# Accumulating DMAs issued from GpSimd in place of VectorE subtractions and sums, in a hybrid encoder layer

## The chip, the cores and the metric

The kernel runs on one core of a Trainium2 chip. The metric is the device time of one execution in microseconds (us), the median of several runs. Beside the runs there is one profiled execution, from which all durations below come.

The engines are TensorE (PE; its weight loads are listed apart as PEld), VectorE (DVE), ScalarE (ACT), GpSimd (POOL) and SyncE (SP, which here issues DMAs only). Each works through its own queue of instructions in order; an instruction that waits for a semaphore holds up everything behind it in that queue.

## The reference, cut to what matters

One layer over 512 tokens of width 1024: a combined input projection, three token mixers with a gated merge, an output projection, and a gated feed-forward network, all in float32.

```
h = rms_norm(x, norm_mix)
proj = h @ w_in                      # pool | lru | q | k | v | 3 gates, 1024 columns each
y_pool = pool_mixer(u_pool); y_lru = rglru_mixer(u_lru)
y_sb = stick_breaking_attention(rms_norm(q), rms_norm(k), v)
merged = sum over the branches b of sigmoid(g_b + b_gate) * (y_b @ w_branch[b])
x = x + merged @ w_out
x = x + (silu(h2 @ w_ffn_gate) * (h2 @ w_ffn_up)) @ w_ffn_down      # h2 = rms_norm(x, norm_ffn)
```

## The kernel before, in words

**Split products.** The operands of the products have the type float32r (`F32R`, fp32r in the rows). Each is split into a high part, the value written in that type, and a low part, what is left of it; a product is then three matmuls, high x high, high x low and low x high (`mm3`, L225). For weights this is `split_w` (L97): ScalarE copies the raw tile into `whi` (L100), VectorE subtracts `whi` from the raw tile into `wlo` (L101). A tile holds 128 x 1024 values, 512 KB.

**Weight tiles and buffers.** All weights up to the feed-forward network go through one list, `specs`: each entry loads a raw tile from memory (SyncE's queue), splits it and hands the two parts to the products. The pool `wp` has three buffers for each of `raw`, `whi` and `wlo`, and `weights` (L218) keeps three entries ahead of the products. So a new high part waits until TensorE is done with the tile three entries back, and a new raw load waits until the split three entries back has read its buffer. `emit_next` (L209) gives these loads and splits a higher priority than the code around them; a scheduler then puts the instructions of each engine into a fixed order when the program is built. What is moved or added in one place can therefore change the order of others, on any engine.

**The q, k and v products.** They use a scheme with seven products in place of eight (Strassen in Winograd's form). For each of q, k and v (`t` = 0, 1, 2) the weights are cut into four blocks 11, 12, 21, 22, and the seven left operands are, in `ORDER` (L130): 11, 12, S2, S1, S3, S4, 22. S3 = 11 - 21, S2 = 22 - S3, S1 = 21 + 22, S4 = 12 - S2. Each block comes in two halves (`i`), so there are fourteen tiles for each `t`, twelve matmuls for each tile. The raw blocks lie in buffers of their own (`qraw`, eight buffers of the tag `w`); S3, S1 and S4 are formed in place of their first operand, S2 in a buffer of another tag. `SUMS_AT` (L153) says at which of the fourteen tiles each sum is written into the program. `qkv_sum` (L144) forms them on VectorE (L149). The results of a product are collected on ScalarE and VectorE (`snap` L718, `final` L722). For q and k a root follows: a sum of squares on VectorE (`ssq`, L679, L680), a power on GpSimd (`rsqq`, L255), four short VectorE operations (L256 to L259), and for k eight scalings on ScalarE (L694). The tensors then go to memory from GpSimd's queue (`qd`, L671), as the gates (`gd`, L502) and the recurrence (`yd`, L613) do. Half chunks of the third gate are mixed in between the products.

**Pool, attention and branches.** Here the eight attention heads run as small tasks between the chunks of the pool and branch products. A branch product (`branch` L862, and L1007 for the third) multiplies a mixer's output by `w_branch`: three branches, four chunks of 256 columns, two half chunks each, so 24 weight tiles, each with 24 matmuls (`half_chunk`, L276). They are entered by `add_branch` (L118) through `add_chunk256` (L111) and `add_direct` (L104).

The functions that the change touches, and what calls them:

Of the kernel before, what the change touches and what calls it, by code (L numbers as in the profile page):

```python
# [8 lines left out]
F32 = mybir.dt.float32  # L9
F32R = mybir.dt.float32r  # L10
BF16 = mybir.dt.bfloat16
AF = mybir.ActivationFunctionType
ALU = mybir.AluOpType
# [3 lines left out]
P = 128  # L17
# [46 lines left out]
def layer_kernel(ctx: ExitStack, tc: tile.TileContext, x, xt, vecs, w_in, w_pool, w_rg, w_ig,  # L64
                 w_branch, w_out, w_fg, w_fu, w_fd, out):
    nc = tc.nc
    act = nc.scalar.activation
# [13 lines left out]
    def b4(shape, name, tag="b", dt=F32):  # L81
        bufs = {"w": NAW, "t": NAT, "b": NAB}[tag]
        return pools["ap0"].tile([P] + shape, dt, tag=tag, name=name, bufs=bufs)
# [5 lines left out]
    def cols(ap, k0, nk, c0, nc_):  # L89
        return ap[k0 * P:(k0 + nk) * P, c0:c0 + nc_].rearrange("(k p) c -> p k c", p=P)  # L90


    def weight_tiles(nh, nl, o=0):
        return [wp.tile([P, 1024 + 128], F32R, tag=tag, name=n)[:, o:o + 1024]
                for tag, n in (("whi", nh), ("wlo", nl))]

    def split_w(raw, shape, n):  # L97
        hi, lo = (t.rearrange("p (a b) -> p a b", a=shape[1])
                  for t in weight_tiles("whi" + n, "wlo" + n))
        act(hi, raw, AF.Copy)  # L100
        dve.tensor_tensor(lo, raw, hi.bitcast(F32), ALU.subtract)  # L101
        return hi, lo

    def add_direct(key, src, a, b):  # L104
        def make(n):
            raw = wp.tile([P, a, b], F32, tag="raw", name="raw" + n)
            nc.sync.dma_start(raw, src)
            return split_w(raw, [P, a, b], n)
        specs.append((key, make))

    def add_chunk256(key, ap, c0):  # L111
        add_direct(key + (0,), cols(ap, 0, 4, c0, 256), 4, 256)
        add_direct(key + (1,), cols(ap, 4, 4, c0, 256), 4, 256)
# [18 lines left out]
    CH = {"11": 0, "12": 0, "21": 1, "22": 1}  # L132
    KH = {"11": 0, "12": 1, "21": 0, "22": 1}
    qraw = {}

    def qkv_raw(t, nm, i):
        if (t, nm, i) not in qraw:
            qraw[t, nm, i] = r = b4([2, 512], f"qw{t}{nm}{i}", "w")
            nc.sync.dma_start(r, cols(w_in, 4 * KH[nm] + 2 * i, 2, 2048 + t * 1024 + CH[nm] * 512, 512))
        return qraw[t, nm, i]  # L140

    def qkv_sum(t, nm, i):  # L144
        x, y, op = {"S3": ("11", "21", ALU.subtract), "S2": ("22", "S3", ALU.subtract),
                    "S1": ("21", "22", ALU.add), "S4": ("12", "S2", ALU.subtract)}[nm]
        x, y = qkv_raw(t, x, i), qkv_raw(t, y, i)
        r = b4([2, 512], f"qs{t}{i}") if nm == "S2" else x
        dve.tensor_tensor(r, x, y, op)  # L149
        qraw[t, nm, i] = r  # L150
# [5 lines left out]
    def add_seven(t, nm, i):  # L156
        def make(n):
            p = 2 * ORDER.index(nm) + i
            if p < 4:
                qkv_raw(t, nm, i)  # L160
            h, l = None, None
            if p == 1:
                h, l = split_w(qraw[t, nm, i], [P, 2, 512], n)
            if p in SUMS_AT:
                qkv_sum(t, *SUMS_AT[p])
            return (h, l) if h is not None else split_w(qraw[t, nm, i], [P, 2, 512], n)
        specs.append((("seven", t, nm, i), make))
# [6 lines left out]
    for n in range(4):  # L174
        add_direct(("first", n), cols(w_in, 2 * n, 2, 5120, 512), 2, 512)
# [158 lines left out]
    with ExitStack() as first:  # L334
# [379 lines left out]
        for t in range(3):  # L714
            ps = {}
            r = {}
# [301 lines left out]
    with ExitStack() as ffn:  # L1018
# [3 lines left out]
        def g4(shape, name, dt=F32):  # L1022

            return gp.tile([P] + shape, dt, tag="g", name=name)
# [13 lines left out]
        for c in range(4):  # L1038
# [5 lines left out]
            for j in range(2):  # L1044
# [3 lines left out]
                t = x1p[c // 2, j][:, c % 2, :]  # L1048
# [77 lines left out]
        CH = {"11": 0, "12": 0, "21": 1, "22": 1}  # L1126
        KH = {"11": 0, "12": 1, "21": 0, "22": 1}
# [3 lines left out]
        raw = {}  # L1131
# [81 lines left out]
        for c in range(NDIRECT):  # L1213
# [4 lines left out]
            a = g4([2, S], f"act{c}")  # L1218
# [26 lines left out]
        for m in range(4):  # L1245
            t = fp.tile([P, 2, S], F32, tag="mm", name=f"ps_d{m}")
# [38 lines left out]
        for kc in range(KD, last + 1):  # L1285
            split_act(kc + 1)
            ah, al = split.pop(kc)
            for e in range(2):
# [3 lines left out]
                for j in range(4):  # L1292
# [5 lines left out]
                    if kc == last:  # L1298
                        t = x1[m]
# [8 lines left out]
        for q in range(2):  # L1308
# [4 lines left out]
            lo, hi, full = slice(0, H), slice(H, S), slice(0, S)  # L1313
# [50 lines left out]
```

## Time and profile before

| what | value |
|---|---|
| median of 3 runs | 936.94 us (936.89 to 939.02) |
| profiled execution: its own time | 936.89 us |
| profiled execution: span from first to last instruction | 934.8 us |
| granted TensorE clock, mean | 0.999 |
| DMA packets | 124.13 MB, mean 133 GB/s |

A view with groups gives line, engine, operation, out<-in by the program's names, shapes and count, then the busy time in us and the mean of one in ns, then the idle time of the engine just before them and what ended it. A timeline row gives start and duration in us, then the instruction; the bracket gives the idle time before it and the releaser. A DMA issue's row ends with the median time from issue to landing. A row of the chain that ended last gives start, duration and a run of instructions. Matmuls overlap, and their ends are modelled, so a wait of TensorE is a little longer than the idle time shown.

### The profile page before, as it was taken

To read this page: it belongs to the slowest core of one execution; us is meant where nothing else is said; L and a number is where in the kernel's file an instruction comes from. 1 tells how busy PE (TensorE), PEld (TensorE's weight loads), DVE (VectorE), ACT (ScalarE), POOL (GpSimd) and SP (SyncE) were. 2 spreads that over 40 slices of the span, in tenths; PEclk is the share of its full clock that TensorE was granted. 3 is DMA by queue.
4 is the path that set the end of the run, shared out by engine and by line. 5 is a ranking of instruction groups with operands and counts; after the bars stand their busy time and mean duration, and the time that the engine had idled before them with its cause. 6 is when DMAs were issued, how large, how long until landed. Compare 5 with 4: busy or idle time off the path is not lost.

```text
span 934.8 us, 13035 instructions
## 1 busy us (share of the span) xinstructions
PE 922.3 (99%) x5089; PEld 793.8 (85%) x5089; DVE 709.8 (76%) x889; ACT 485.7 (52%) x657; POOL 44.4 (5%) x69
## 2 busy tenths in 40 slices
PE   9999999999999999999999999999999999999998
PEld 6887787787878888788788878889999999988898
DVE  6897599786686698867865545699888888787465
ACT  6636977545574556645633324454555555653232
POOL 2000000322211000000000000000000000000000
PEclk9999999999999999999999999999999999999999
DMA  9574352743614933255532344355433334533001
GB/s 336 157 263 125 105 189 68 246 137 117 199 72 150 292 113 106 89 157 173 145 100 84 100 135 135 93 149 143 135 92 104 101 110 135 164 100 103 1 29 63
DMA packets 126894, 124.13 MB, mean 133 GB/s; under 512 B 7408, under 2 KB 105712, under 8 KB 126832
## 3 DMA queue, kind: packets, MB, share of 16 engines
q1 hardware_dynamic: 122800, 108.87, 38.0%
q0 software_dynamic: 3888, 14.16, 4.4%
q8 instruction: 40, 0.66, 0.3%
q10 hardware_dynamic: 144, 0.26, 0.1%
q14 instruction: 22, 0.18, 0.1%
HBM read 107.02 MB, written 16.25 MB: 132 GB/s over the span
## 4 chain that ended last, share of the span: by engine, by line
PE 86%; DVE 7%; ACT 2%; issue 2%; POOL 2%; DMA 0%; SPq 0%; POOLq 0%; DVEq 0%; ACTq 0%
PE ps_y L1176 11%; PE ps_x L1176 8%; PE ps_br L226 5%; PE ps_br L228 4%; PE ps_br L227 4%; PE ps_q L708 4%; PE ps_d L226 3%; PE ps_d L228 3%; PE ps_d L227 3%; PE ps_gate L226 2%; PE ps_gate L227 2%; PE ps_gate L228 2%; PE ps_dy L1176 2%; PE ps_gate L627 2%; DVE wlo L101 2%
## 5 line engine op out<-in xcount | busy, mean ns | idle before, releaser
L100 ACT ACTIVATE whi<-raw 128x1024 fp32r<-128x1024 f32 x93 | 98.4, 1058 | 150.0 <-PE ps_br L227 46.2
L101 DVE TENSOR_TENSOR wlo<-raw,whi 128x1024 fp32r<-128x1024 f32 x93 | 113.5, 1221 | 65.4 <-ACT whi L100 60.3
L1166 ACT ACTIVATE wh_S<-w_S 128x1024 fp32r<-128x1024 f32 x44 | 46.6, 1061 | 56.5 <-PE ps_y L1176 25.6
L1167 DVE TENSOR_TENSOR wl_S<-w_S,wh_S 128x1024 fp32r<-128x1024 f32 x44 | 53.6, 1221 | 12.8 <-ACT wh_S L1166 12.6
L1166 ACT ACTIVATE wh<-w 128x1024 fp32r<-128x1024 f32 x33 | 35.0, 1062 | 49.1 <-issue 13.2
L101 DVE TENSOR_TENSOR wlo<-qw,whi 128x1024 fp32r<-128x1024 f32 x36 | 43.9, 1221 | 17.0 <-ACT whi L100 16.9
L1167 DVE TENSOR_TENSOR wl<-w,wh 128x1024 fp32r<-128x1024 f32 x33 | 40.3, 1222 | 17.4 <-ACT wh L1166 17.4
L100 ACT ACTIVATE whi<-qw 128x1024 fp32r<-128x1024 f32 x36 | 38.0, 1055 | 23.6 <-PE ps_q L708 15.0
L226 PE MATMUL ps_gate<-HH,whi 128*128 128x512 f32 x128 | 50.2, 392 | 0.0
L227 PE MATMUL ps_gate<-HL,whi 128*128 128x512 f32 x128 | 49.8, 389 | 0.0
L228 PE MATMUL ps_gate<-HH,wlo 128*128 128x512 f32 x128 | 49.8, 389 | 0.0
L226 PE MATMUL ps_d<-ah,whi 128*128 128x512 f32 x112 | 43.7, 391 | 0.0
L227 PE MATMUL ps_d<-al,whi 128*128 128x512 f32 x112 | 43.6, 389 | 0.0
L228 PE MATMUL ps_d<-ah,wlo 128*128 128x512 f32 x112 | 43.6, 389 | 0.0
L1154 DVE TENSOR_TENSOR w_S<-w,w 128x1024 f32<-128x1024 f32 x22 | 26.9, 1223 | 3.3 <-PE ps_d L227 2.9
L226 PEld LDWEIGHTS ps_gate<-HH,whi 128*128 128x128 f32 x128 | 24.0, 188 | 5.6 <-issue 0.7
L228 PEld LDWEIGHTS ps_gate<-HH,wlo 128*128 128x128 f32 x128 | 24.0, 188 | 5.0
L227 PEld LDWEIGHTS ps_gate<-HL,whi 128*128 128x128 f32 x128 | 24.0, 188 | 4.9
L1154 DVE TENSOR_TENSOR w_S<-w,w_S 128x1024 f32<-128x1024 f32 x22 | 26.9, 1223 | 0.6
L929 DVE TENSOR_TENSOR_SCAN E<-K,zero 128x511 f32<-128x511 f32 (+3 forms) x32 | 25.5, 811 | 1.1 <-ACT K L924 1.1
L226 PE MATMUL ps_out<-mth,whi 128*128 128x512 f32 x64 | 25.0, 390 | 0.9 <-DVE g L311 0.9
L226 PE MATMUL ps_br<-yph,whi 128*128 128x512 f32 x64 | 25.6, 400 | 0.0
(633 smaller groups left out, 3004.7 us busy)
## 6 DMA issues: line engine op xcount, KB each, us to landing
raw<-in_w_in_dram SPq DMA_DIRECT2D x39, 512.0 KB, 4.7
qw<-in_w_in_dram SPq DMA_DIRECT2D x24, 512.0 KB, 5.0
raw<-in_w_branch_dram SPq DMA_DIRECT2D x24, 512.0 KB, 3.5
w<-in_w_ffn_gate_dram SPq DMA_DIRECT2D x36, 256.0 KB, 3.7
w<-in_w_ffn_up_dram SPq DMA_DIRECT2D x36, 256.0 KB, 4.3
raw<-in_w_ffn_down_dram SPq DMA_DIRECT2D x14, 512.0 KB, 3.6
qd<-r POOLq DMA_DIRECT2D x12, 512.0 KB, 3.4
at<-qd SPq DMA_DIRECT2D x24, 256.0 KB, 5.1
```

Source lines behind the costliest of these rows:

```text
L100: act(hi, raw, AF.Copy)
L101: dve.tensor_tensor(lo, raw, hi.bitcast(F32), ALU.subtract)
L226: nc.tensor.matmul(ps, lh, rh, start=start, stop=False, skip_group_check=skip)
L227: nc.tensor.matmul(ps, lh, rl, start=False, stop=False, skip_group_check=skip)
L228: nc.tensor.matmul(ps, ll, rh, start=False, stop=stop, skip_group_check=skip)
L627: nc.tensor.matmul(pss[n // 2][n % 2], w[:, k % 2, n * P:(n + 1) * P], hu[k][x_], start=k == 0 and w is wh and x_ == 0, stop=k == KT - 1 a ...
L708: nc.tensor.matmul(ps[:, a, :], b_[:, k, ts_], a_[:, kk, :], start=first and n == k == 0, stop=n == 2 and k == 3, skip_group_check=True)
L929: dve.tensor_tensor_scan(E[:, f - 1:c0 + n - 1][:, ::-1], K[:, f:c0 + n][:, ::-1], zero[:, 0:1].to_broadcast([P, c0 + n - f]), 1.0, ALU.mu ...
L1154: dve.tensor_tensor(t, raw[c, x], raw[c, y], op)
L1166: act(h, raw[c, nm], AF.Copy)
L1167: dve.tensor_tensor(l, raw[c, nm], h.bitcast(F32), ALU.subtract)
L1176: nc.tensor.matmul(o, a[:, w, k, :], b[:, k, :], start=first and n == k == 0, stop=n == 2 and k == 3, skip_group_check=True)
```

## The change

A new function, `split_d`, makes a weight tile's two parts without VectorE. ScalarE writes the high part, then writes its negative into the low part's buffer; a DMA from GpSimd's queue then adds the raw tile to it in place (`accum_op`), so that the buffer ends as raw - high. `add_direct` uses it for the entries whose key begins with `br`, the 24 branch tiles; all others keep `split_w`.

In `qkv_sum`, S1 = 21 + 22 is no longer a VectorE addition of two raw blocks: a DMA from GpSimd's queue reads block 22 from memory and adds it to the buffer of block 21. Block 22 is still loaded as before, for S2 and for its own product. There are six such tiles, two for each of q, k and v. The other three sums stay on VectorE.

```diff
+    def split_d(raw, shape, n):
+        hi, lo = (t.rearrange("p (a b) -> p a b", a=shape[1])
+                  for t in weight_tiles("whi" + n, "wlo" + n))
+        act(hi, raw, AF.Copy)
+        act(lo, hi.bitcast(F32), AF.Copy, scale=-1.0)
+        nc.gpsimd.dma_start(lo, raw, accum_op=ALU.add)
+        return hi, lo
+
     def add_direct(key, src, a, b):
         def make(n):
             raw = wp.tile([P, a, b], F32, tag="raw", name="raw" + n)
             nc.sync.dma_start(raw, src)
-            return split_w(raw, [P, a, b], n)
+            return (split_d if key[0] == "br" else split_w)(raw, [P, a, b], n)
         specs.append((key, make))
...
     def qkv_sum(t, nm, i):
+        if nm == "S1":
+            qraw[t, nm, i] = r = qkv_raw(t, "21", i)
+            src = cols(w_in, 4 * KH["22"] + 2 * i, 2, 2048 + t * 1024 + CH["22"] * 512, 512)
+            nc.gpsimd.dma_start(r, src, accum_op=ALU.add)
+            return
         x, y, op = {"S3": ("11", "21", ALU.subtract), "S2": ("22", "S3", ALU.subtract),
-                    "S1": ("21", "22", ALU.add), "S4": ("12", "S2", ALU.subtract)}[nm]
+                    "S4": ("12", "S2", ALU.subtract)}[nm]
```

## The prediction

> **What bounds the kernel now.** I read the page's totals first, then the busy time of two stretches, then the waits of TensorE, then the timeline around each of them. In the stretches the columns are the time, then the busy us of TensorE, of its weight loads, of VectorE, ScalarE and GpSimd; in the waits who waited for whom, the us in total, how often, the longest.
>
> ```profile
> span 934.8 us, 13035 instructions
> ...
> PE 922.3 (99%) x5089; PEld 793.8 (85%) x5089; DVE 709.8 (76%) x889; ACT 485.7 (52%) x657; POOL 44.4 (5%) x69
> ...
> q0 software_dynamic: 3888, 14.16, 4.4%
> ```
> ```profile
> 131.00:300.00 169.00, 165.19 (x722) 134.82 (x721) 132.87 (x155) 104.19 (x135) 35.52 (x32) 1.00 0.44 146
> 300.00:545.00 245.00, 243.34 (x1208) 200.90 (x1207) 177.10 (x272) 118.83 (x201) 0.00 (x0) 1.00 0.46 135
> ```
> ```profile
> PE ps_q L708 <- DVE wlo L101: 3.0, 3, 1.4
> ...
> PE pw L943 <- DVE ypl L838: 0.9, 1, 0.9
> ...
> PE ps_q1S L708 <- DVE wlo L101: 0.8, 2, 0.5
> ```
>
> TensorE is busy for 922.3 of 934.8 us, and its instructions don't change. So the change acts only through idle time of TensorE: what it takes away, or what it adds. In the stretch of the q, k and v products (131 to 300) TensorE is idle for 169.0 - 165.2 = 3.8 us, and the waits say why: 3.0 + 0.8 us for a low part (wlo) that VectorE delivers late. In the whole pool, attention and branch stretch (300 to 545) it is idle for 245.0 - 243.3 = 1.7 us, and no wait in the whole list names the low part of a branch weight. VectorE is the busiest helper in both (132.9 of 169, 177.1 of 245), but only in the first does it hold TensorE up.
>
> **Part one: the branch weights' low parts.** Each of the 24 half chunks now costs VectorE one subtraction; the change puts a second ScalarE activation (the negated high part) and one accumulating DMA from GpSimd in its place.
>
> ```profile
> L101 DVE TENSOR_TENSOR wlo<-raw,whi 128x1024 fp32r<-128x1024 f32 x93 | 113.5, 1221 | 65.4 <-ACT whi L100 60.3 <-PE pq L892 5.0
> L100 ACT ACTIVATE whi<-raw 128x1024 fp32r<-128x1024 f32 x93 | 98.4, 1058 | 150.0 <-PE ps_br L227 46.2 <-PE ps_out L227 26.0 <-PE ps_d L227 21.1
> 421.61 1.06 ACT L100 ACTIVATE whi<-raw 128x1024 fp32r<-128x1024 f32 x1 [4.38 <-PE ps_br L227]
> 427.05 1.06 ACT L100 ACTIVATE whi<-raw 128x1024 fp32r<-128x1024 f32 x1 [4.38 <-PE ps_br L227]
> 422.71 1.23 DVE L101 TENSOR_TENSOR wlo<-raw,whi 128x1024 fp32r<-128x1024 f32 x1 [4.21 <-ACT whi L100]
> qd<-r POOLq DMA_DIRECT2D x12, 512.0 KB, 3.4
> gd<-gt POOLq DMA_DIRECT2D x11, 512.0 KB, 5.4
> ```
>
> VectorE loses 24 x 1.22 = 29.3 us of its 177.1; ScalarE gains, at the price of the high part's row, 24 x 1.06 = 25.4 us on its 118.8; GpSimd, empty here (the second stretch's 0.00), gains 24 issues. None of the three becomes the bound of 245 us. What matters is the time from the high part to the landed low part. The two ScalarE rows show the tight rhythm: each high part starts when TensorE lets go of the buffer three tiles back (the releaser), and the next follows after 427.05 - 421.61 = 5.44 us, one tile on TensorE (24 matmuls, 0.227 us each). With three buffers the tile whose high part starts at T is due at T + 2 x 5.44, and its low part two matmuls later, at T + 11.3. Until now it is ready at 422.71 + 1.23 - 421.61 = 2.3 us after T. Afterwards ScalarE is through both activations at 2 x 1.06 = 2.1, 2.3 with a hand-over like the one to VectorE, and 9.0 us are left for the DMA from issue to landing.
>
> The trace has no accumulating DMA. Below, it can't beat a plain store of the same 512 KB from GpSimd, 3.4 us; above, I take the slower of the two store rows twice, 2 x 5.4 = 10.8. A plain GpSimd DMA keeps 16 engines busy for 4.4% x 934.8 / 27 issues (12 + 11 on the rows here, four more yd stores) = 1.5 us; reading a second operand adds that once more, so I take 3.4 + 1.5 = 5, nearer to the lower row because the branch stretch's queues are not crowded. It is hidden under two tiles of matmuls: 0 us on the path. The bounds: under 9.0 nothing, at 10.8 a rival below.
>
> Two queues wait with it. The raw buffer is let go when the DMA has read it, some 4 us later than now, and SyncE's next branch load, with the gate, head and recurrence loads behind it, starts that much later. And what stands behind a negation on ScalarE comes 1.06 us later.
>
> ```profile
> 501.34 16.75 SPq L107 DMA_DIRECT2D raw<-in_w_branch_dram  x4
> raw<-in_w_branch_dram SPq DMA_DIRECT2D x24, 512.0 KB, 3.5
> 371.25 1.06 ACT L100 ACTIVATE whi<-raw 128x1024 fp32r<-128x1024 f32 x1
> 373.28 0.69 ACT L895 ACTIVATE qkh<-pq,vt 128x512 fp32r<-128x512 f32 x1 [0.97 <-PE py L227]
> ```
>
> Four such loads are issued over 16.75 us, one a tile; a buffer comes round in three tiles, 16.3 us, less 2.3 for the split and 3.5 for the load: 10.5 us to spare, so 4 cost nothing. ScalarE's tightest place is near 373, ahead of the two short waits of TensorE behind the pooling; there the negation falls into 0.97 us in which ScalarE waits for TensorE (py) anyway: 371.25 + 2 x 1.06 = 373.4 in place of 373.3. Without that cover it would cost its 1.06. I take 0.
>
> The Trainium skill, "Collectives: The Full Stack", section on the bandwidth ceiling, says an adding DMA isn't slowed by its adder but by its two source reads on one ring, which halves its rate. No run here shows it yet. By that rule the 1.5 us would become 3.0, the sum would stay as it is, and a late landing would be less likely than I put it below.
>
> **Part two: the S1 sums.** Six of the twelve additions and differences of this row leave VectorE, 6 x 1.22 = 7.3 us; six accumulating DMAs read the second operand from memory once more.
>
> ```profile
> L149 DVE TENSOR_TENSOR qw<-qw,qw 128x1024 f32<-128x1024 f32 x12 | 14.5, 1219 | 0.1
> 263.88 11.20 PE ps_q L708 x47
> 280.52 5.44 PE ps_q L708 x24
> ```
>
> Their landing is covered: a tile of these products takes TensorE 5.44 / 2 = 2.72 us, and the tightest of the six, the second of v, is issued near 261 and due five tiles after the v tile at 263.1 to 263.9, near 276.7: 15 us, beyond even the 10.8. What costs is the order. In the changed program, set beside the old one engine by engine, VectorE, ScalarE and GpSimd have another order, and each runs its queue strictly in turn. So I replayed by hand the four places where TensorE waits for a low part, with the old durations; a long VectorE operation follows the last at 1.14 us (208.40 after 207.26, below).
>
> ```profile
> 150.23 1.22 DVE L101 TENSOR_TENSOR wlo<-qw,whi 128x1024 fp32r<-128x1024 f32 x1
> 167.30 1.22 DVE L603 TENSOR_TENSOR ls<-ls,li 128x1024 f32<-128x1024 f32 x1
> 168.43 1.21 DVE L101 TENSOR_TENSOR wlo<-qw,whi 128x1024 fp32r<-128x1024 f32 x1
> 173.67 1.22 DVE L101 TENSOR_TENSOR wlo<-qw,whi 128x1024 fp32r<-128x1024 f32 x1
> 167.48 3.69 POOL L255 TENSOR_TENSOR rsqq<-ssq,mhalf 128x8 f32<-128x8 f32 x1 [3.66 <-DVE ssq L680]
> 272.09 1.66 POOL L255 TENSOR_TENSOR rsqq<-ssq,mhalf 128x8 f32<-128x8 f32 x1 [10.90 <-DVE ssq L680]
> ```
>
> First, q's second tile (low part at 150.23, TensorE waits until it ends): a sum leaves the stretch ahead of it, but the second of the two products of L602 moves up into the gap; five long operations stand ahead before and after. 0 us.
>
> Second, q's first S3 tile (low part at 173.67). The root on GpSimd (L255) takes 1.66 us while VectorE does nothing long, but here 3.69, ending 1.5 us after VectorE's last two-operand operation (171.17 against 168.43 + 1.21 = 169.64). In the new order the low part that was at 168.43 stands behind the wait for that root and a scan: root done near 170, scan to 171.3, low part done at 172.5 and due at 170.7, 1.8 us late, the next another 0.25. 2.05 us in place of 1.55 (the longest wait, 1.4, and what the modelled ends hide): +0.5.
>
> ```profile
> 207.26 1.22 DVE L149 TENSOR_TENSOR qw<-qw,qs 128x1024 f32<-128x1024 f32 x1
> 208.40 1.21 DVE L101 TENSOR_TENSOR wlo<-qw,whi 128x1024 fp32r<-128x1024 f32 x1
> 223.61 2.16 ACT L694 ACTIVATE r<-r,krs 128x128 f32<-128x128 f32 x7 [3.20 <-DVE krs L259]
> ```
>
> Third, k's S1 tiles (0.8 shown). A wait for a root now stands ahead of the low part at 208.40 too, just behind S4's sum (207.26, by the relief now at 206.4): root done at 207.6 + 1.5 = 209.1, low part at 209.3. The relief is gone again, and three of the eight scalings (L694) now stand before the S1 tile's high part on ScalarE. I get the low part at 225.0, due 224.0, and 0.5 more on the next, against 1.1 today: +0.5.
>
> ```profile
> 256.87 1.22 DVE L101 TENSOR_TENSOR wlo<-qw,whi 128x1024 fp32r<-128x1024 f32 x1
> 258.90 1.25 ACT L501 ACTIVATE gt<-ps_gate,vt 128x512 f32<-128x512 f32 x2
> 263.54 1.06 ACT L100 ACTIVATE whi<-qs 128x1024 fp32r<-128x1024 f32 x1 [1.66 <-PE ps_q L708]
> 264.51 1.00 ACT L720 ACTIVATE r<-ps_q 128x1024 f32<-128x1024 f32 x1
> 273.71 0.75 POOL L671 DMA_DIRECT2D qd<-r  x1
> ```
>
> Fourth, the start of v. GpSimd gets both S1 transfers ahead of k's last root, and that root waits in the queue behind the second, which waits for the second S3 difference (260.5: the low part at 256.87, a reduction, the difference). Issue 0.75 us, as for a store, to 261.3; a low part on VectorE until 261.8, so the root ends at 263.3, its four short operations at 264.1. On ScalarE the eight scalings that need it, the gate pair and a copy now come ahead of the first S2 high part: 2.4 + 1.25 + 1.0 gives a start at 268.8 in place of 263.54. It is done at 269.8, due at 268.5; its low part at 271.2, due at 270.3. 1.35 + 0.95 = 2.3 us, less the 0.2 that is waited at 263.88 now: +2.1. The unknown here is the issue: below, the store's 0.75; above, twice that for the second operand, which adds 0.5. I take the store's.
>
> **The sum.** 0 (branches) + 0 + 0.5 + 0.5 + 2.1 = +3.1 us. The profiled execution took 936.89 us with a span of 934.8, and the median of the runs is 936.94, so both bases agree: **940.0 us**. A measurement of this kernel can tell about 0.3%, or 2.8 us, from no change.
>
> **Rivals.** *The relief pays (not slower).* If GpSimd's root is done before VectorE and ScalarE come to wait for it, the 7.3 us off VectorE remove the waits on low parts: 3.0 + 0.8, and 0.9 of the pooling wait (pw on ypl), 4.7 us: 932.2. For it: these waits all name VectorE. Against it: at three of the four places the new order puts a wait for the root ahead. *The new order is absorbed.* Each of my four places is a difference of some 1 us between long sums; if they average out, 936 to 939.5, near 938. *Late landings.* If a DMA takes 12 us instead of 5, each low part is 3 us late for its tile, once per round of three tiles. About ten tiles run at the 5.44 us rhythm (those near 421 and those from 501 on), three rounds: 9 us on top, 949; at 20 us, 11 us late a round, some 33. For it: nothing in the trace has such a DMA, and its destination type is not its source type. Against it: it would need over 9 us, well beyond 5.4. *The change doesn't do what it says*: excluded for the count; the order of the program shows 30 subtractions and sums gone and 30 transfers added.
>
> **How the numbers follow.** Forecast 40% (937.5 to 943.5, decided by the four places, a little over a quarter of it within 0.3%), relief pays 18%, absorbed 22%, late landings 20%. Faster 0.19, same 0.29, slower 0.52. The range takes in the relief and late landings to three rounds: 932.5 to 950.
>
> **What would show it.** Right: the wait of the v products' ps_q on ScalarE's high part near 269, the last k root starting only after the second S1 transfer's issue, and no wait in the branch products on wlo. Wrong in part one if branch products wait on a DMA of wlo, or if its issue to landing exceeds 9 us; wrong in part two if TensorE's idle time from 131 to 300 is below 3.8 us.

## The result, and the profile after

The changed kernel takes 940.77 us, median of 7 runs (939.17 to 941.38), beside 938.36 us for the kernel before on the same chip (7 runs, 936.89 to 939.44): a ratio of 1.0025, 95% interval 1.0014 to 1.0036. It is slower by 0.25%, some 2.3 us. The profiled execution took 939.17 us against 936.89. The runs of the kernel before, and of nearly every other kernel here, lie in two groups some 2 us apart (the kernel before in the last session: 936.7 to 937.1 and 938.4 to 939.6), which come from TensorE's first microseconds (last section); ratios are taken over both groups, and what is read from two traces is counted from 100 us on.

The page of the changed kernel, totals and GpSimd's DMA queue (line numbers behind `qkv_sum` are 14 higher than before: the subtraction is still L101, the negation L109, the branch transfer L110, the S1 transfer L157, the root L269, the scalings L708, the copy in `snap` L734):

```profile
span 937.4 us, 13111 instructions
...
PE 922.9 (98%) x5089; PEld 793.5 (85%) x5089; DVE 676.1 (72%) x859; ACT 509.6 (54%) x681; POOL 70.4 (8%) x99
...
q0 software_dynamic: 8976, 29.89, 13.9%
```

VectorE is 33.7 us lighter (709.8 to 676.1), and the span 2.6 us longer; TensorE's own work is the same. The two stretches (time, then busy us of TensorE, its weight loads, VectorE, ScalarE, GpSimd), and TensorE's waits:

```profile
131.00:300.00 169.00, 163.25 (x712) 132.70 (x712) 126.23 (x148) 102.97 (x133) 39.73 (x35) 1.00 0.55 161
300.00:545.00 245.00, 243.30 (x1206) 200.60 (x1205) 148.87 (x248) 143.23 (x226) 21.81 (x27) 1.00 0.74 187
```
```profile
PE ps_q L722 <- DVE wlo L101: 2.2, 2, 1.4
PE ps_q0S L722 <- DVE wlo L101: 1.6, 1, 1.6
PE ps_q L722 <- ACT whi L100: 1.2, 1, 1.2
PE pw L957 <- DVE ypl L852: 0.9, 1, 0.9
PE ps_q1S L722 <- DVE wlo L101: 0.8, 1, 0.8
```

In the first stretch TensorE now idles 169.0 - 163.25 = 5.75 us in place of 3.8, in the second 1.7 as before: the loss lies in the q, k and v products. There is no wait on a branch low part. VectorE has 148.87 us of work in the second stretch (177.1 before), ScalarE 143.23 (118.8). New is a wait on ScalarE's high part. It is one place, the start of v, here in the timeline (start, duration, engine, line, and in brackets the idle time ahead and who ended it), sorted by time:

```profile
261.06 0.16 DVE L694 TENSOR_SCALAR ssq<-ssq 128x8 f32<-128x8 f32 x1
261.37 1.22 POOL L157 DMA_DIRECT2D qw<-in_w_in_dram  x1 [3.42 <-DVE ssq L694]
262.15 2.14 POOL L269 TENSOR_TENSOR rsqq<-ssq,mhalf 128x8 f32<-128x8 f32 x1
264.33 0.17 DVE L270 TENSOR_TENSOR krs<-rsqq 128x8 f32<-128x8 f32 x1 [1.97 <-POOL rsqq L269]
265.20 2.46 ACT L708 ACTIVATE r<-r,krs 128x128 f32<-128x128 f32 x8 [0.56 <-DVE krs L273]
267.56 1.24 ACT L515 ACTIVATE gt<-ps_gate,vt 128x512 f32<-128x512 f32 x2
268.70 1.01 ACT L734 ACTIVATE r<-ps_q 128x1024 f32<-128x1024 f32 x1
269.61 2.00 ACT L100 ACTIVATE whi<-qs 128x1024 fp32r<-128x1024 f32 x2
270.70 0.51 PE L722 MATMUL ps_q<-whi,hT2h 128*128 128x512 f32 x1 [1.18 <-ACT whi L100]
271.96 0.51 PE L722 MATMUL ps_q<-wlo,hT2h 128*128 128x512 f32 x1 [0.76 <-DVE wlo L101]
```

k's last root (L269) gets its sum of squares at 261.2, and VectorE waits 1.97 us for it (264.33). ScalarE then scales k (L708), finishes a gate pair and a copy, and only then makes v's first S2 high part (269.61, before: 263.54). TensorE waits 1.18 us for it, then 0.76 for the low part.

To place the loss exactly I took, for each matmul, its start in this trace less the start of the same matmul in the trace before (the median of five neighbours, less the same at 100 us; times are those of the trace before). The changed kernel is late by 0.33 us at 180, 0.56 at 240, 0.07 at 268, 2.33 at 275 and 295, 2.57 at 500 and 2.56 at 930. So q costs 0.33, k 0.23, the old wait at 263.9 gives back 0.49, the start of v costs 2.26, and everything behind 300 costs 0.23.

The new DMAs (number, KB, median us from issue to landing), with two groups of the attention and output stages below them, then those two in the kernel before:

```profile
wlo<-raw POOLq DMA_DIRECT2D x24, 512.0 KB, 5.6
qw<-in_w_in_dram POOLq DMA_DIRECT2D x6, 512.0 KB, 6.0
g<-gd SPq DMA_DIRECT2D x22, 256.0 KB, 5.5
raw<-in_w_out_dram SPq DMA_DIRECT2D x8, 512.0 KB, 5.1
```
```profile
g<-gd SPq DMA_DIRECT2D x22, 256.0 KB, 2.9
raw<-in_w_out_dram SPq DMA_DIRECT2D x8, 512.0 KB, 3.5
```

### The profile page after: what moved, and what is told of

It is laid out like the page before. It is cut to its first block, busy times and chain, and to the rows that moved or that the text cites. A ratio compares the mean times of both kernels' runs of the same rounds, so it can differ in the third digit from the quotient of the medians.

```text
span 937.4 us, 13111 instructions
## 1 busy us (share of the span) xinstructions
PE 922.9 (98%) x5089; PEld 793.5 (85%) x5089; DVE 676.1 (72%) x859; ACT 509.6 (54%) x681; POOL 70.4 (8%) x99
## 3 DMA queue, kind: packets, MB, share of 16 engines
q0 software_dynamic: 8976, 29.89, 13.9%
## 4 chain that ended last, share of the span: by engine, by line
PE 87%; DVE 6%; ACT 3%; issue 2%; POOL 1%; DMA 0%; SPq 0%; ACTq 0%; DVEq 0%; POOLq 0%
PE ps_y L1190 11%; PE ps_x L1190 8%; PE ps_q L722 5%; PE ps_br L241 4%; PE ps_br L242 4%; PE ps_br L240 4%; PE ps_d L240 3%; PE ps_gate L240 3%; PE ps_d L241 3%; PE ps_gate L241 3%; PE ps_d L242 3%; PE ps_gate L242 3%; PE ps_dy L1190 2%; PE ps_gate L641 2%; DVE wlo L101 2%; PE ps_dx L1190 2%
## 5 line engine op out<-in xcount | busy, mean ns | idle before, releaser
L101 DVE TENSOR_TENSOR wlo<-raw,whi 128x1024 fp32r<-128x1024 f32 x69 | 84.2, 1221 | 44.7 <-ACT whi L100 40.4
L101 DVE TENSOR_TENSOR wlo<-qw,whi 128x1024 fp32r<-128x1024 f32 x36 | 43.9, 1222 | 21.1 <-ACT whi L100 21.1
L110 POOL DMA_DIRECT2D wlo<-raw x24 | 20.7, 863 | 214.6 <-ACT wlo L109 155.6
L325 DVE TENSOR_TENSOR g<-ps_br,g 128x512 f32<-128x512 f32 x16 | 11.0, 689 | 27.5 <-PE ps_br L242 27.5
```

## The experiments

The table has each kernel's ratio to the kernel before with its 95% interval, and its lateness against it in us, worked out as above.

| label | what it is | ratio | at 180 | 240 | 268 | 275 | 295 | 930 |
|---|---|---|---|---|---|---|---|---|
| (changed kernel) | | 1.0025 (1.0014 to 1.0036) | 0.33 | 0.56 | 0.07 | 2.33 | 2.33 | 2.56 |
| e1_branch_only | S1 on VectorE | 1.0002 (0.9992 to 1.0011) | -0.01 | -0.02 | -0.02 | -0.03 | -0.03 | 0.14 |
| e2_s1_only | branches on VectorE | 1.0024 (1.0015 to 1.0032) | 0.31 | 0.52 | 0.02 | 2.32 | 2.32 | 2.35 |
| e3_s1_q_k | v's S1 on VectorE | 1.0005 (0.9996 to 1.0014) | 0.35 | 0.57 | 0.58 | 0.56 | 0.56 | 0.72 |
| e4_root_behind | k's last root held back | 1.0013 (1.0004 to 1.0022) | 0.35 | 0.58 | 0.09 | 0.58 | 1.52 | 1.68 |
| e5_root_ahead | v's second transfer held back | 1.0022 (1.0012 to 1.0033) | 0.32 | 0.57 | 0.99 | 2.18 | 2.18 | 2.35 |
| e6_twice | two transfers a branch tile | 1.0411 (1.0392 to 1.0429) | 0.32 | 0.52 | 0.03 | 2.29 | 2.29 | 39.25 |
| e7_second_of_v | v's second S1 alone | 1.0013 (1.0003 to 1.0023) | 0.00 | 0.00 | 0.01 | 1.60 | 1.60 | 1.62 |
| e8_pool_too | branch and pool low parts | 1.0111 (1.0093 to 1.0129) | -0.02 | 0.02 | 0.02 | 0.04 | 0.04 | 11.91 |
| e9_holds | three roots held back | 1.0004 (0.9994 to 1.0015) | -0.87 | -0.27 | -0.76 | -0.24 | 0.68 | 0.85 |
| e10_holds_before | the same, no transfers | 1.0041 (1.0026 to 1.0057) | -0.67 | -0.14 | -0.13 | -0.11 | 2.87 | 2.93 |
| e11_two_holds | two roots held back, no transfers | 0.9987 (0.9977 to 0.9997) | -0.66 | -2.06 | -1.32 | -1.36 | -1.36 | -1.32 |
| e12_two_holds_s1 | the same, S1 of q and k by transfer | 0.9982 (0.9973 to 0.9992) | -0.87 | -1.99 | -1.25 | -1.29 | -1.29 | -1.25 |

**The two parts apart.** e1 takes the `S1` branch out of `qkv_sum`, e2 gives the branches `split_w` back.

```
# e1
             "S1": ("21", "22", ALU.add), "S4": ("12", "S2", ALU.subtract)}[nm]
# e2
-            return (split_d if key[0] == "br" else split_w)(raw, [P, a, b], n)
+            return split_w(raw, [P, a, b], n)
```

> Only the branch weights' low parts go through GpSimd's accumulating transfers; the S1 sums are back on VectorE. Theory (the loss sits in the q, k and v products): TensorE idles 3.8 us from 131 to 300 as in the kernel before, no wait of TensorE on a branch low part, span 0 to +0.5 us of the kernel before, ratio 0.9995 to 1.001. Rival one (the 24 transfers or their second operand's traffic slow the attention loads or the low parts): +1.5 to +3 us, behind 300. Rival two (relief of VectorE pays in this stretch): -1 us or more.

> Only the six S1 sums go through accumulating transfers; the branch low parts are back on VectorE. Theory: TensorE idles 5.7 us from 131 to 300 as in the changed kernel, the time is +2 to +2.7 us of the kernel before, with the wait on ScalarE's first S2 high part of v near 271. Rival (the two parts need one another, for instance by buffers or by queues): less than +1.5 us, the rest appears only with both.

The two stretches of e1:

```profile
131.00:300.00 169.00, 165.19 (x722) 134.87 (x721) 134.38 (x156) 104.56 (x136) 34.47 (x29) 1.00 0.44 147
300.00:545.00 245.00, 243.31 (x1207) 200.82 (x1206) 148.38 (x247) 143.88 (x226) 21.68 (x27) 1.00 0.73 188
```

Idle 3.8 and 1.7 us, as in the kernel before, with VectorE at 148.4 of 245: 24 transfers and 28.7 us of relief change nothing that can be told. e2 has the whole loss, 2.35 us, with the same wait on the high part near 271. The parts don't need one another; the loss is the S1 sums'.

**v's sums back.** The condition becomes `nm == "S1" and t < 2`.

> Both parts of the change, but v's two S1 sums are back on VectorE. Theory (most of the loss is at the start of v): the fourth place falls away, TensorE's wait near 271 on the first S2 high part of v is gone, the shift against the kernel before at 300 is +0.3 to +0.6 us (the q and k places), the time +0.3 to +0.9. Rival (the q and k places carry it, or the first queue delays grow later): +2 us or more stays.

0.56 us at 295 and 0.72 at the end, as the theory had it; the wait on v's high part is gone.

**Queue or order?** Two kernels with all 30 transfers, in which one instruction is held back. e4 holds k's last root until v's first S2 sum is there (its code is also put off until that sum exists); e5 holds v's second transfer until the root is there. The held operand takes the other one times zero, so no value changes.

```
# e4, ahead of rsqrt in post2
+            if (t, i, j) == (1, 1, 0):
+                dve.scalar_tensor_tensor(s_[:, 0:1], qraw[2, "S2", 0][:, 0, 0:1], 0.0, s_[:, 0:1],
+                                         ALU.mult, ALU.add)
# e5, ahead of the transfer in qkv_sum; lastrs["t"] is the last root
+            if (t, i) == (2, 1):
+                dve.scalar_tensor_tensor(r[:, 0, 0:1], lastrs["t"][:, 0, 0:1], 0.0, r[:, 0, 0:1],
+                                         ALU.mult, ALU.add)
```

> All of the change, but k's last root is held until the first S2 sum of v is made: its sum of squares takes that sum's first column times zero. All six S1 transfers stay. Theory 'the order on VectorE and ScalarE' (VectorE stands idle for the root ahead of the S2 sums, and ScalarE scales k ahead of the first S2 high part): the wait near 271 falls away, the time is 1.5 to 2.2 us under the changed kernel. Theory 'GpSimd's queue' (the root is late because it stands behind the second transfer): the root is not earlier, so nothing is gained, the time is as in the changed kernel or above.

> All of the change, but v's second S1 transfer is held until k's last root is done (its destination's first element takes the root times zero). The order on VectorE and ScalarE is else that of the changed kernel; only GpSimd's queue has the root ahead of the transfer. Theory 'the order on VectorE and ScalarE': the root still waits for its sum of squares at 261.2 and for VectorE's long operation behind it, so it ends 0.4 us earlier at most; the time is 0 to 0.4 us under the changed kernel and the wait near 271 stays. Theory 'GpSimd's queue' (as predicted): the root ends 1.2 us or more earlier, and the time is 1.2 to 2 us under the changed kernel.

e5 first: its timeline on VectorE and GpSimd (all of it some 2.5 us later than above, since this execution started later; the transfer is L160, the root L272).

```profile
263.53 0.16 DVE L698 TENSOR_SCALAR ssq<-ssq 128x8 f32<-128x8 f32 x1
263.85 1.66 POOL L272 TENSOR_TENSOR rsqq<-ssq,mhalf 128x8 f32<-128x8 f32 x1 [3.44 <-DVE ssq L698]
266.01 1.24 POOL L160 DMA_DIRECT2D qw<-in_w_in_dram  x1 [0.50 <-DVE krs L275]
```

The root goes ahead of the transfer, and starts only when its sum of squares is there (263.53 + 0.16), as it did before. It ends at 265.51; less the 2.47 us by which this execution was later already at 100 us, at 263.04 against 264.29 above. So the queue did delay the root, by up to 1.25 us, as the second theory had it, but the time is as the first one had it: 2.18 late at 275 against 2.33. VectorE hands the gain back: in this order a low part stands between the root's four short operations, and it comes so late that TensorE waits for it near 268 (the 0.99 of the table). With the low part ahead, as in the changed kernel, the root would end 1.5 us behind it (262.4), at 263.9, 0.4 us earlier; whether these 0.4 would reach TensorE stays open. e4 takes the wait near 271 away (0.58 at 275), but gives 0.94 back at 280.4, in a wait for ScalarE's copy (L742) that stands behind six of the eight scalings (L716):

```profile
PE ps_q L730 <- ACT r L742: 0.6, 1, 0.6
```
```profile
278.14 1.85 ACT L716 ACTIVATE r<-r,krs 128x128 f32<-128x128 f32 x6
279.90 1.04 ACT L100 ACTIVATE whi<-qw 128x1024 fp32r<-128x1024 f32 x1
280.85 0.99 ACT L742 ACTIVATE r<-ps_q 128x1024 f32<-128x1024 f32 x1
```

So the order theory was right on the place, wrong on the gain: 0.88 us at 930 in place of 1.5 to 2.2, because the scalings now stand in the way at another place.

**One transfer alone.** The kernel before with `nm == "S1" and (t, i) == (2, 1)`.

> Only one of the 30 transfers: v's second S1 sum; all else as in the kernel before. GpSimd's queue has this transfer ahead of k's last root, as in the changed kernel, but ScalarE keeps the first S2 high part of v ahead of the scaling of k, and VectorE the S2 sum ahead of the root's operations. Theory 'the order on VectorE and ScalarE': 0 to +0.6 us of the kernel before. Theory 'GpSimd's queue': the root is late behind the transfer and with it what follows, +1.5 us or more.

It costs 1.62 us, which is the queue theory's number, but by neither theory's road. The wait is on `snap`'s copy:

```profile
PE ps_q L722 <- ACT r L734: 1.5, 1, 1.5
```
```profile
263.10 1.26 POOL L157 DMA_DIRECT2D qw<-in_w_in_dram  x1 [6.26 <-DVE krs L272]
266.26 0.16 DVE L694 TENSOR_SCALAR ssq<-ssq 128x8 f32<-128x8 f32 x1
266.58 2.49 POOL L269 TENSOR_TENSOR rsqq<-ssq,mhalf 128x8 f32<-128x8 f32 x1 [1.47 <-DVE ssq L694]
269.97 2.45 ACT L708 ACTIVATE r<-r,krs 128x128 f32<-128x128 f32 x8 [0.20 <-DVE krs L273]
272.33 1.00 ACT L734 ACTIVATE r<-ps_q 128x1024 f32<-128x1024 f32 x1
```

The transfer (263.10) has long been issued when the root gets its sum of squares (266.26 + 0.16), so the root doesn't wait for it. But with one sum less on VectorE, the program's order has the sum of squares, the root and the eight scalings one step earlier than in the kernel before, and the scalings now stand ahead of the copy on which TensorE waits. In the kernel before this root started at 272.09, here at 266.58, or 264.1 without the 2.44 us by which this execution was later already at 100 us. What costs is where the scalings fall. That the scheduler moves them because VectorE has less to do, and not because a transfer now makes the sum, is read from the orders; no run here tells the two apart.

**How much landing time there is.** e6 makes each branch low part by two transfers, e8 makes the pool weights' low parts by transfer too (S1 on VectorE).

```
# e6
-        act(lo, hi.bitcast(F32), AF.Copy, scale=-1.0)
-        nc.gpsimd.dma_start(lo, raw, accum_op=ALU.add)
+        act(lo, hi.bitcast(F32), AF.Copy, scale=-2.0)
+        for _ in range(2):
+            nc.gpsimd.dma_start(lo, raw, accum_op=ALU.add)
# e8
-            return (split_d if key[0] == "br" else split_w)(raw, [P, a, b], n)
+            return (split_d if key[0] in ("br", "pool") else split_w)(raw, [P, a, b], n)
```

> All of the change, but each branch low part comes by two accumulating transfers one after the other: minus twice the high part, plus the raw weights, plus the raw weights again (so the low part is doubled). Issue to the second landing is then 0.9 + 5.6 + 5.6 = 12 us and more. Theory (9.0 us of slack per tile at the tight rhythm of 5.44 us, none of it used before): TensorE now waits for branch low parts, about 3 us once per round of three tiles near 421 and from 501 on, in all 6 to 15 us over the changed kernel. Rival (the raw buffers or the high parts are made earlier than I think, the slack is larger): within 1 us of the changed kernel. Rival (GpSimd's queue, held by the first landing, delays the next tile's transfer too, so that the delays add up): over 20 us.

> Low parts of the branch weights and of the eight pool weight tiles by accumulating transfers, the S1 sums on VectorE. It asks whether a relief of VectorE can pay where VectorE does hold TensorE up (0.9 us for ypl and 0.5 us behind it near 384 to 387). Theory (landing 5.6 us fits under two tiles): 0 to -1.4 us of the kernel before. Rival (the tiles at the seam of the stages are made too late for 5.6 us of landing): +2 us or more, with a wait of ps_pool on a low part.

TensorE's waits in e6, with GpSimd's timeline there (L111 are the transfers) and two of TensorE's waits:

```profile
PE ps_br L243 <- DMA wlo<-raw: 25.1, 15, 4.7
```
```profile
529.84 1.75 POOL L111 DMA_DIRECT2D wlo<-raw  x2 [6.33 <-DMA wlo<-raw]
537.63 1.75 POOL L111 DMA_DIRECT2D wlo<-raw  x2 [6.04 <-DMA wlo<-raw]
534.44 0.50 PE L243 MATMUL ps_br<-ys4h,wlo 128*128 128x512 f32 x1 [0.70 <-DMA wlo<-raw]
542.46 0.50 PE L243 MATMUL ps_br<-ys0h,wlo 128*128 128x512 f32 x1 [2.28 <-DMA wlo<-raw]
```

976.14 us, some 35 over the changed kernel: the rival in which the delays add up. A pair in GpSimd's timeline is not one tile's: its first member is the second transfer of a tile, which waits until that tile's first has landed (the releaser), and its second member is the first transfer of the next tile, which stands behind it in the queue. The pair at 529.84 shows it: the second transfer of one tile lands for the matmul at 534.44, and the tile begun behind it, at 530.4, has its second transfer issued at 537.63 and is there for the matmul at 542.46. So from first issue to second landing a tile takes 12 us, as expected. But the queue stands still for the landing of each first transfer, and tiles follow each other every 537.63 - 529.84 = 7.79 us in place of 5.44. The waits are 25.1 of the 39.25 - 2.56 = 36.7 us that TensorE is later than in the changed kernel. Some 8 more are half pace: its granted clock is 0.51 from 428 to 435 and 0.50 for some 3.3 us each from 527.1, 551.0 and 575.0 (last section).

e8 loses 11.9 us between 295 and 350, where the rival saw it:

```profile
PE ps_pool L242 <- DMA wlo<-raw: 5.6, 2, 3.9
```

Here the raw buffers are the short supply. Loads of pool weights are issued at 302.12, 315.18 and 319.01, each less than 0.1 us after the landing of an accumulating transfer that reads a raw buffer (302.06, 315.16, 318.99), and ScalarE stands idle 9.6 us until 306.13 for such a load. The waits near 384 to 387, which the relief was to remove, are still there, some 12 us later (0.5 and 0.9 us).

**The order set right.** If the place of the roots is what costs, roots held behind what TensorE needs next should cost nothing. e9 (all of the change) and e10 (none of it) hold three roots, each by the sum of squares taking a column of the low part named here times zero, with the root's code put off until that tile exists:

```
# e9, e10
+    HOLD = {(0, 0, 0): (0, "S1", 1), (1, 0, 0): (1, "S1", 1), (1, 1, 0): (2, "S2", 1)}
...
+            if (t, i, j) in HOLD:
+                low = lows[HOLD[t, i, j]].bitcast(F32)
+                dve.scalar_tensor_tensor(s_[:, 0:1], low[:, 0, 0:1], 0.0, s_[:, 0:1],
+                                         ALU.mult, ALU.add)
# e11, e12
+    HOLD = {(0, 0, 0): (0, "S1", 1), (1, 0, 0): (1, "S3", 0)}
```

> All of the change, and three roots held on VectorE's queue behind the low part that TensorE waits for next: q's first root behind the low part of q's second S1 tile, k's first behind k's second S1 tile, k's last behind v's second S2 tile (each time the sum of squares takes the low part's first column times zero). Theory (the change costs because the relief of VectorE lets roots, and k's scalings with them, move up ahead of what TensorE waits for): q's and k's places lose their waits (1.65 us near 172.5, 0.76 near 225.7), v's falls away, and the relief pays at last: -0.5 to -2.5 us of the kernel before. Rival (waiting for GpSimd costs wherever it is put, or the scalings collide later): the time stays 1 us or more above the kernel before.

> The kernel before with the same three holds, and without any accumulating transfer. It tells what the holds bring alone. If the relief of VectorE (six S1 sums) is what pays under the holds: 0 to -0.7 us of the kernel before here, and e9_holds lies below it. If the holds alone bring it: as e9_holds.

Neither theory's number held. e9's rival had the cause, scalings that collide later, though the 0.85 us at 930 falls short of its 1. Both win in q (-0.87 and -0.67 at 180), and lose it again: k's first scalings now stand ahead of the copy that frees the bank for S3 (a loss of 1.8 and 1.9 us at 230.7), and the last ones ahead of the copy at 280. e10's ratio is the roughest of the table, as its runs spread from 939.4 to 943.9 us. e10 has 4.3 us of waits for that copy, e9 2.1:

```profile
PE ps_q L736 <- ACT r L748: 2.1, 2, 1.5
```
```profile
PE ps_q L722 <- ACT r L734: 4.3, 2, 2.7
```

So I moved the second hold behind k's first S3 tile, where the copy comes first, and left v as it was:

> The kernel before, no accumulating transfer, with two holds: q's first root behind the low part of q's second S1 tile, and k's first root behind the low part of k's first S3 tile, so that k's eight scalings come after the copy (snap) that frees the bank for S3. Theory (a root and its scalings cost when they stand ahead of what TensorE waits for, and nothing when they stand behind it): TensorE's shift against the kernel before is -0.6 us after 175 as in e10_holds_before, -1.6 to -1.9 us at 228, and now stays there, as nothing is changed in v: -1.2 to -1.9 us in all. Rival (the scalings collide wherever they are put): 0 to +1.5 us, with a new wait on a copy of ScalarE after 228.

> The same two holds, and the S1 sums of q and k by four accumulating transfers; v and the branches as in the kernel before. If a relief of VectorE by four sums (4.9 us) pays once no root stands in the way: below e11_two_holds by 0.3 us or more. If VectorE's relief was never the point: within 0.3 us of e11_two_holds. If GpSimd's longer queue costs by itself: above it.

Both beat the kernel before, e11 as its theory had it: e11 by 0.13% (937.49 us beside 938.48), e12 by 0.18% (936.20). TensorE's idle time from 131 to 300 is 169 - 166.39 = 2.6 us in e12, and nothing waits for a copy there:

```profile
131.00:300.00 169.00, 166.39 (x727) 135.80 (x727) 130.56 (x155) 105.11 (x136) 37.47 (x36) 1.00 0.54 161
```
```profile
PE ps_q L736 <- DVE wlo L101: 2.6, 3, 1.4
```

e12's median is 1.3 us under e11's, but the intervals overlap, and the traces differ by less than 0.1 us at the end (-1.32 and -1.25). Some 0.4 us of the two times' difference lie outside the span: the profiled executions took 937.76 us for a span of 935.6 and 935.37 for 933.6. So four sums off VectorE add nothing to the two holds that can be told. Of the gain of 2.0 us at 240 some 0.7 go at 263.9, where TensorE, now earlier, waits for a low part of v.

## Why the prediction was right, point by point

**The bound.** That the change acts only through TensorE's idle time holds: its busy time is 922.9 against 922.3, its idle time from 131 to 300 rose by 1.94 us, that from 300 to 545 by 0.04.

**Part one, 0 us.** e1 shows it: 0.14 us at the end, and a ratio whose interval holds 1. The estimate of 5 us from issue to landing was near: 5.6 in the median, and 4.5 to 8.8 over the 24, all under the 9.0 that I had worked out as slack. VectorE's and ScalarE's loads in the stretch came out within 1.1 us of the sums. The second operand's price was right too: (13.9% x 937.4 - 4.4% x 934.8) / 30 = 2.97 us of 16 engines for each transfer, against 1.5 for a plain one. By the rule of the Trainium skill that I had set beside it ("Collectives: The Full Stack", section on the bandwidth ceiling, which states it for a ReduceScatter between cores) it would be 3.0, and the trace agrees; that the cause is the two source reads is not shown here. I had not foreseen that other transfers land later beside them (gate loads 5.5 us for 2.9, output weights 5.1 for 3.5); nothing waits for these. That the raw buffers come free later cost nothing at the branches, as worked out; at the pool weights it is what costs (e8).

**Part two.** Landing was covered, as worked out. The four places:
- First, 0: the wait is 1.42 us in both traces.
- Second, +0.5: I had the low part done at 172.5, and it is (171.29 + 1.20); it cost 0.33. The row that I gave for a root with nothing long on VectorE beside it (272.09, 1.66 us) has two long operations there (L723 at 271.85, a low part at 272.98); the roots at 185.27 and 241.13 in the trace before do stand alone, and take 1.66 us. Nor does a root always end 1.5 us behind the last long operation: in e7 it ends at 266.58 + 2.49 = 269.07, 0.4 us behind a low part.
- Third, +0.5: mis-sized, 0.23. I had the low part done at 225.0 (it was 225.6) and another 0.5 for the next; that one held TensorE up by 0.1 only (done at 228.6, in use at 228.64), since TensorE had already been held up.
- Fourth, +2.1: 2.26 less the 0.49 that is no longer waited at 263.9 (I had 0.2), so 1.77. The high part starts at 269.6 (268.8 by my replay). The issue was mis-sized, 1.22 us and not the store's 0.75, within the bound of 1.5.

The four measured places and the 0.23 behind 300 add up to 2.56 us in the traces (2.3 by the runs), for +3.1. That the absolute 940.0 lies so near the 940.77 is in part luck: the base of 936.94 was the median of three runs, and the kernel before took 938.36 beside the changed one.

**The reason given for the fourth place was only half of it**: that the root "waits in the queue behind the second" transfer. It does, but with the transfer out of its way e5 got 0.15 us of 2.26 back; e7 lost 1.6 us with a root that no transfer delays, and e10 2.9 without any transfer, with scalings ahead of a copy both times. What decides is the other half of the replay, that the scalings, the gate pair and the copy come ahead of the high part: the changed program's order has the root and all that hangs on it earlier. I argued from the queue of the engine that was given work, when most of the cost came from the order on the others.

**The rivals.** *Relief pays* didn't come, and e11 and e12 show why: what could be had here (1.3 us) lay in the order, and is there without any relief. (Its 932.2 lay just below the range that was to take it in.) *Absorbed* holds for the branches alone. *Late landings* had no chance to show: the slowest of the 24 took 8.8 us, only just under the 9.0. I had given 12 us from issue to landing a price of 9 us, once a round of three tiles. e6, with 12 us, lost some 37 in the traces, but in it GpSimd's queue waits for a landing too, so that the rhythm of 5.44 us is the limit there, and not the slack of 9.0. In the changed kernel a branch transfer's issue waits for ScalarE's negation and never for a landing, so what a single late transfer would cost was not tested.

## What to carry to other kernels

Taking work off an engine that is not the bound can move what stands behind it to an earlier place, and where queues run in order an early block that nobody needs (here eight scalings for a store) can stand ahead of one that the bound engine waits for: look at what moves up, not only at what goes away. Before paying for relief, try holding the unneeded block back; here two such holds brought 0.13%, and the transfers nothing beyond it that can be told. The accumulating DMAs of the branches were free because their landings (4.5 to 8.8 us) fitted into the slack of 9.0 and nothing else waited for them. Where GpSimd's queue had to wait for a landing (e6), or the next load for a raw buffer (e8), they cost 37 and 12 us.

## What the runs showed of the hardware

The issue of an accumulating transfer of 512 KB holds GpSimd 0.86 us from one buffer on the chip into another (the group of the changed kernel; the last number of the middle column is the mean in ns) and 1.22 to 1.26 us from memory (rows above), where a store of that size took 0.75.

```profile
L110 POOL DMA_DIRECT2D wlo<-raw x24 | 20.7, 863 | 214.6 <-ACT wlo L109 155.6
```

A long wait costs TensorE more than its length. In e8 it waits 3.9 us (the longer of the two above) until 315.2, and then runs at a granted clock of 0.50 until near 319 (columns as in the stretches above; the clock stands behind GpSimd's number):

```profile
308.00:311.00 3.00, 3.00 (x19) 2.52 (x17) 1.13 (x2) 3.00 (x5) 0.86 (x1) 1.00 1.21 290
316.00:318.00 2.00, 2.00 (x7) 1.54 (x6) 0.00 (x0) 0.00 (x0) 0.00 (x0) 0.50 1.08 222
```

Matmuls start 0.43 us apart there, 0.227 otherwise; waits of up to 1.65 us in the changed kernel show nothing like it. The Trainium skill, "TensorE: Matmul & The Clock Gate", section "What's actually happening", says that the clock halves after an idle window of about 3.4 us and comes back after as long a busy one. The wait of 3.9 us and the half pace of some 3.4 us behind it agree, but shorter waits brought it too. In e8 it comes back behind waits of 1.33 and 0.29 us (at 320.69 and 321.48):

```profile
322.00:325.00 3.00, 3.00 (x9) 2.24 (x9) 1.86 (x5) 1.07 (x3) 0.73 (x1) 0.59 1.15 304
```

In e6 waits of 2.1, 1.8 and 2.1 us brought half pace (from 527.1, 551.0 and 575.0), one of 2.3 us, until 542.46, didn't. So a wait need not be as long as that window; what decides is not shown.

TensorE's start shows half pace too. Its first four matmuls on real data take 1.20 us in the trace before and 2.07 in that of e1, behind a pause of about the same length, and the half pace lasts until about 9 us; from then on e1's matmuls are 1.83 us late, and stay so. Of the 13 traces set against the one before, six are at most 0.33 us late at 100 us, and seven 1.83 to 2.54:

```profile
5.28 1.20 PE L627 MATMUL ps_gate<-hu,whi 128*128 128x512 f32 x4 [0.65 <-ACT hu L363]
```
```profile
5.46 2.07 PE L641 MATMUL ps_gate<-hu,whi 128*128 128x512 f32 x4 [0.83 <-ACT hu L377]
```
